# Two more units by seven products in an FFN output stage, another order, and an earlier look-ahead for the last weights

## The chip, the cores and the metric

The kernel runs on one core of a Trainium2 chip. The metric is the device time of one execution in microseconds; where several runs are given, their median counts.

## What is computed

One layer of a decoder: a sparse attention mixer, then a SwiGLU FFN, with RMSNorm ahead of each and at the end. The change lies in the second half of the FFN and in nothing else:

```python
def swiglu(h, w_in, w_out):          # h: 512 x 2048
    z = h @ w_in                     # w_in: 2048 x 11264
    a, b = z[..., :D_FF], z[..., D_FF:]
    return (jax.nn.silu(a) * b) @ w_out     # D_FF = 5632; w_out: 5632 x 2048
```

All data is float32. The kernel keeps float32 accuracy on TensorE by splitting each operand into a high part (rounded to the type that TensorE takes) and a low part (the rest), and adding three products: high by high, high by low, low by high. This is the helper `three`, lines 272 to 274, so every product appears as three matmuls.

## The kernel before

**Units.** The FFN output multiplies the gated activations `a` (512 tokens by 5632) by `w_out`. The 5632 rows are cut into 22 *pairs* of 2 x 128 rows, and the 2048 output columns into 4 *blocks* of 512. A *unit* is one pair in one block, 88 in all; `ORDER[b]` lists the pairs of block b in the order in which they are worked. TensorE goes through the units one after the other. In block 3 the last `N_TAIL` = 4 pairs of the order (17, 19, 20, 21) are held back: they are worked token tile by token tile at the very end, so that a finished tile can be normalised and stored while the next is multiplied.

**Two forms of a unit.** A plain unit (`plain_tile`, L1248) is 4 token tiles x 2 halves x 3 = 24 matmuls with 512 columns. A unit listed in `SEVEN[b]` (`seven_unit`, L1255) treats tokens and columns as a 2 x 2 block matrix and uses seven products of half size in place of eight, 42 matmuls with 256 columns. It needs sums of the activation's quarters and sums of the weight's quarters:

- The activation's side of a seven (seven quarter-sized matrices, high and low, tiles `ah` and `al`) is made once, by `form` (L1188), in the unit's first block. `form` is a generator of three steps, taken four, three and two units ahead of its unit; it reads the plain data by a SyncE transfer (`load_form`) into a part of `acc` that is not in use yet.
- The pairs in `KEPT` stay in SBUF for all blocks. The others are *passing*: `form` stores `ah` and `al` to DRAM (`d_s`, L1214, on the Pool queue), and later blocks fetch them back (`load_seven`, L1231, L1239, also on the Pool queue), 896 KB each. The pool `ast` has two buffers for passing pairs, so a fetch or a `form` waits until TensorE has left the passing pair before the last.
- The weight's side is made for every unit by `weight_sums` (L1125): four sums into the tile `tt`, then a split into `thi` and `tlo` (L1139 on ScalarE, L894 on VectorE), of which there are two buffers.

`merge_sums` (L1270) adds the four accumulators that the sevens of a block share into `acc`, once, in the unit after the block's last seven: one ScalarE copy and six VectorE instructions.

**Weights.** `W2` loads each unit's 512 KB of weights by SyncE (L77, tile `raw`, `RAW` = 3 buffers) and splits them into `whi` (ScalarE, L93) and `wlo` (VectorE, L95), in `CONV` = 4 buffers. `take(k)` sees to it that the weights of this unit and of the next k are split, and then issues loads for the next three that are not:

```python
    def ahead(self, n):
        last = len(self.specs)
        while self.ncv < min(self.nt + n, last):
            if self.nd <= self.ncv:
                self.load()
            self.split()
        while self.nd < min(self.ncv + RAW, last):
            self.load()
```

**Plain activations.** A plain unit's activation comes from DRAM (`d_a`) into one of two single buffers, `rawx` or `tt` (`load_a`, L1102, SyncE, L1108), and is split by `split_a` (L1110, L1116 on ScalarE, then L894). `tt` is the same tile in which `weight_sums` works, so a plain activation gets it only after the sums of the last seven ahead of it are split. For the last four pairs the split goes to `ah` and `al`.

**The order of the queues** is the order in which the program issues: each engine, and each DMA queue with it, works its instructions one after the other and waits where one has to wait. For one unit the loop of the output stage issues `W2.take`, then `split_a` up to the next unit (further ahead in the last two units before the held pairs), then `merge_sums` if it is due, the steps of `form`, the matmuls, `load_seven`, and one step of `ready`, which prepares the norm of the block before.

Of the kernel before, what the change touches and what calls it, by code (L numbers as in the profile page):

```python
# [29 lines left out]
N_PLAIN = 3  # L30
N_TAIL = 4
KEPT = (3, 8, 13, 16, 18)
SEVEN = [KEPT + x for x in ((6, 11), (6, 11, 0, 1, 2, 4)) + 2 * ((6, 11, 0, 1, 2, 4, 5, 7),)]
ORDER = [tuple(range(22)),
# [3 lines left out]
TP_GAP, HN_GAP = 40, 48  # L38
RESYNC = 14
SPREAD = 2560  # L40
# [128 lines left out]
def nsa_block(ctx: ExitStack, tc: tile.TileContext, x, rel_bias, mix_g, ffn_g, fin_g, w_in, w_out,  # L169
# [649 lines left out]
    def add(t, cb, p):  # L819
        a = acc[:, t, 512 * cb:512 * (cb + 1)]  # L820
        dve.tensor_tensor(a, a, p, op=OP.add)
# [13 lines left out]
    with tc.tile_pool(name="n2", bufs=1) as n2:  # L835
# [8 lines left out]
        for cb in (2, 3):  # L844
            po = out_tiles()
            for i in range(6):
                w = W.take(2 if cb == 2 else min(2 + i, 6))
# [206 lines left out]
    with tc.tile_pool(name="tmp", bufs=1) as tmp:  # L1054
# [10 lines left out]
        for p in range(N_PLAIN):  # L1065
            if p:
                pa = [ps3.tile([128, 512], F32, name="pp") for _ in range(2)]
                for i in range(4):
                    w = W.take()
# [17 lines left out]
    W2 = Weights(nc, rawp, convp, specs2)  # L1087
# [7 lines left out]
    for n, (b, j) in enumerate(seq):  # L1095
        home = "tt"
        if j not in SEVEN[b]:
            home = min(free, key=free.get)
# [11 lines left out]
    def split_a(n):  # L1110
        if n in held:
            if n >= NU - N_TAIL:
                h, l = (asl.tile([128, 1792], F32R, name=f"a{x}")[:, 48:48 + 2 * S] for x in "hl")
            else:
                h, l = (tp.tile([128, 1600], F32R, name=f"t{x}")[:, :2 * S] for x in ("hi", "lo"))
            act(h, a_raw[n], AF.Copy)  # L1116
            sub(l, a_raw.pop(n), f32(h))
            a_hl[n] = h, l
        elif n < NU:
            a_hl[n] = seven[seq[n][1]] if seq[n][1] in KEPT else passing.pop(0)  # L1120
        load_a(n)
# [3 lines left out]
    def weight_sums(n):  # L1125

        def first(r):
            b11, b12, b21, b22 = (r[:, 256 * i:256 * (i + 1)] for i in range(4))
            ttf = tp.tile([128, 1536], F32, name="tt", bufs=1)[:, :768]
            c0 = 0 if n and seq[n - 1][1] in SEVEN[seq[n - 1][0]] else 32  # L1130
            tt = ttf.rearrange("p (n c) -> p n c", n=3)
            sub(tt[:, 0], b22, b12)
            sub(b12, b12, b11)
            plus(tt[:, 1], tt[:, 0], b11)
            sub(tt[:, 2], b21, tt[:, 1])

            def rest():
                h, l = (tp.tile([128, 1600], F32R, name=f"t{x}")[:, c0:c0 + 768] for x in ("hi", "lo"))
                act(h, ttf, AF.Copy)  # L1139
                sub(l, ttf, f32(h))  # L1140
                t_hl[n] = [x.rearrange("p (n c) -> p n c", n=3) for x in (h, l)]

            return rest

        return first

    for n, (b, j) in enumerate(seq):
        if j in SEVEN[b]:
            W2.sums[n] = weight_sums(n)
# [25 lines left out]
    scratch = [acc[:, :, 1024:1536], acc[:, :, 1536:]]  # L1175
    forms = [n for n, (b, j) in enumerate(seq) if j in SEVEN[b] and (not b or j not in SEVEN[b - 1])]
    visits = [n for n, (b, j) in enumerate(seq) if j in SEVEN[b] and j not in KEPT]

# [52 lines left out]
    def load_seven(n):  # L1231

        while n_visit[0] < len(visits):
            v = visits[n_visit[0]]
            if v in forms or sum(x > n for x in visits[:n_visit[0]]) >= 2:
                break
            h, l = (ast.tile([128, 1792], F32R, name=f"a{x}") for x in "hl")
            for i, x in enumerate((h, l)):
                pool.dma_start(x.bitcast(F32), d_s[seq[v][1], i])  # L1239
            keep_seven(seq[v][1], h, l)  # L1240
            n_visit[0] += 1
# [6 lines left out]
    def plain_tile(n, w, t, first, last):  # L1248
        for k in range(2):
            ah, al = (x[:, S * k:S * (k + 1)][:, tok(t)] for x in a_hl[n])  # L1250
            three(po[t], ah, al, w[0][:, k], w[1][:, k], first and k == 0, last and k == 1)
# [3 lines left out]
    def seven_unit(n, w, first):  # L1255
        b = [[x[:, i, 256 * c:256 * (c + 1)] for x in w] for i in range(2) for c in range(2)]
        th, tl = t_hl.pop(n)
        right = dict(p1=b[0], p5=b[1], p2=b[2], p3=b[3], p7=(th[:, 0], tl[:, 0]), p6=(th[:, 1], tl[:, 1]),
                     p4=(th[:, 2], tl[:, 2]))
        for name in ("p7", "p6", "p1", "p5", "p2", "p3", "p4"):  # L1260
            for u in range(2):
                if name in qs:
                    o, new = qs[name][:, 256 * u:256 * (u + 1)], seq[n][1] == first and u == 0
                else:
                    o = po[2 * (name == "p4") + u][:, 256 * (name == "p3"):][:, :256]
                    new = not started and name != "p3"
                lh, ll = (x[:, L[name], 128 * u:128 * (u + 1)] for x in a_hl[n])
                three(o, lh, ll, *right[name], new, False)

    def merge_sums(b, qs):  # L1270

        c = slice(512 * b, 512 * b + 256), slice(512 * b + 256, 512 * b + 512)
        m = late2.tile([128, 1024], F32, name="m")
        u2, u3 = m[:, :512], m[:, 512:]

        def halves(x):
            return x.rearrange("p (u c) -> p u c", u=2)

        act(u3, qs["p1"], AF.Copy)
        plus(u2, u3, qs["p6"])  # L1280
        plus(acc[:, :2, c[0]], acc[:, :2, c[0]], halves(u3))
        plus(u3, u2, qs["p7"])
        plus(acc[:, 2:, c[0]], acc[:, 2:, c[0]], halves(u3))
        mm2 = m.rearrange("p (a c) -> p a c", a=2)
        plus(mm2, mm2, qs["p5"].unsqueeze(1).to_broadcast([128, 2, 512]))
        plus(acc[:, :, c[1]], acc[:, :, c[1]], m.rearrange("p (t c) -> p t c", t=4))

    def ready(b, gf):

        c = slice(512 * b, 512 * (b + 1))  # L1290
        for t in range(NT):
            junk = late2.tile([128, 1024], F32, name="m")[:, :512]
            act(junk, acc[:, t, c], AF.Square, accum_out=ss[t][:, b:b + 1])
            dve.tensor_tensor(acc[:, t, c], acc[:, t, c], gf, op=OP.mult)
            yield
# [3 lines left out]
    for b in range(4):  # L1299
        units = ORDER[b][:-N_TAIL] if b == 3 else ORDER[b]  # L1300
        po = [pf.tile([128, 512], F32, name=f"f{i}") for i in range(4)]
        qs = {x: pf.tile([128, 512], F32, name=f"f{i}") for i, x in enumerate(("p1", "p5", "p6", "p7"))}
        first7 = next(j for j in units if j in SEVEN[b])
        last7 = [j for j in units if j in SEVEN[b]][-1]
        started = False
        for i, j in enumerate(units):
            left = len(units) - 1 - i if b == 3 else 9
            w = W2.take(max(1, 3 - left))
            while na <= n + 1 + max(0, 2 - left):
                split_a(na)  # L1310
                na += 1
            if pending is not None:
                merge_sums(*pending)
                pending = None
            for k in (1, 2, 3, 4):
                next(forming.get(n + k, iter(())), None)
            if j in SEVEN[b]:
                seven_unit(n, w, first7)
            else:
                for t in range(NT):  # L1320
                    plain_tile(n, w, t, not started, b < 3 and i == len(units) - 1)
            started = True
            if j == last7:
                pending = b, qs
            load_seven(n)
            if i >= 4:
                next(todo, None)
            if i == 12:
                gf = late2.tile([128, 512], F32, name="gf")
                nc.sync.dma_start(gf, fin_g[None, 512 * b:512 * (b + 1)].to_broadcast([128, 512]))  # L1330
            n += 1
        if b < 3:
            for t in range(NT):
                add(t, b, po[t])
            todo = ready(b, gf)
# [50 lines left out]
```

## Time and profile before

| | |
|---|---|
| three runs | 2192.6, 2198.13, 2196.51 us; median 2196.51 |
| the profiled execution | 2191.91 us, span 2190.2 us |
| mean granted TensorE clock | 0.997 |
| output stage | from about 1724 us to the end of the span |

A row of a timeline gives the start in us from the span's start, the time of one instruction (or from the first to the last of several), the engine, the line, the operation, the tile written and the tiles read, and in brackets the idle time before it and what ended it. A row of waits gives who waited for whom, the sum in us, how often, and the longest. Engines: PE is TensorE (PEld its weight load), DVE VectorE, ACT ScalarE, POOL GpSimd, SP SyncE; SPq and POOLq are their DMA queues. Matmuls are pipelined, so what one costs is the distance to the start of the next. In the table by windows the columns are: the stretch, its length, the busy time of PE, PEld, DVE, ACT and POOL with the number of instructions, the granted TensorE clock, the share of the DMA engines, and GB/s.

### The profile page before, as it was taken

What the parts mean: (1) busy time and instruction counts of PE and PEld (TensorE: products, weight loads), DVE (VectorE), ACT (ScalarE), POOL (GpSimd) and SP (SyncE); (2) the same over time, 40 slices, a digit from 0 to 9 for tenths busy, and PEclk for the clock granted to TensorE, in tenths of its full rate; (3) what the DMA queues carried; (4) which work ended last, traced back from release to release, by engine and by line L of the source; (5) the groups of instructions that cost most, each with busy time, mean ns of one, the idle gap of its engine ahead of it and who ended that gap; (6) DMA issues with size and microseconds to landing.
All of it is one profiled execution on the core that took longest, in us unless ns stands there. A gap on an engine that the chain in (4) does not pass through costs nothing.

```text
span 2190.2 us, 37229 instructions
## 1 busy us (share of the span) xinstructions
PE 2146.6 (98%) x15154; PEld 1993.1 (91%) x15154; DVE 1564.2 (71%) x2564; ACT 935.7 (43%) x1447; POOL 121.4 (6%) x140
## 2 busy tenths in 40 slices
PE   6999999999999999999999999999999999999997
PEld 5889898888989888899999999999999888999996
DVE  5455565656645536698888888888888787877776
ACT  5343444544544324344444444344343454544344
POOL 3100000000013012000000000000000000001000
PEclk9999999999999999999999999999999999999999
DMA  5655232232263452244433333443334676878884
GB/s 168 208 142 164 77 97 87 83 96 88 92 211 106 164 178 101 97 145 126 130 121 126 126 118 125 126 135 126 120 122 132 243 280 217 293 273 309 303 302 150
DMA packets 240267, 345.18 MB, mean 158 GB/s; under 512 B 12991, under 2 KB 178911, under 8 KB 238944
## 3 DMA queue, kind: packets, MB, share of 16 engines
q1 hardware_dynamic: 225920, 269.39, 38.4%
q0 software_dynamic: 12880, 70.28, 8.3%
q10 hardware_dynamic: 1296, 3.15, 0.4%
q8 instruction: 118, 1.93, 0.4%
q14 instruction: 53, 0.43, 0.1%
HBM read 299.68 MB, written 48.34 MB: 159 GB/s over the span
## 4 chain that ended last, share of the span: by engine, by line
PE 93%; DVE 3%; DMA 2%; ACT 1%; issue 1%; SPq 0%; POOL 0%; ACTq 0%; DVEq 0%; POOLq 0%
PE f L274 18%; PE f L273 18%; PE f L272 18%; PE proj L272 8%; PE proj L274 8%; PE proj L273 8%; PE pt L739 2%; PE pp L274 1%; PE pp L272 1%; PE pp L273 1%; PE o L274 1%; PE o L273 1%; PE s L272 1%; PE s L274 1%; PE o L272 1%; PE s L273 1%
## 5 line engine op out<-in xcount | busy, mean ns | idle before, releaser
L95 DVE TENSOR_TENSOR wlo<-raw,whi 128x1024 fp32r<-128x1024 f32 (+1 forms) x208 | 252.6, 1217 | 142.9 <-ACT whi L93 141.9
L93 ACT ACTIVATE whi<-raw 128x1024 fp32r<-128x1024 f32 (+1 forms) x226 | 234.4, 1041 | 219.7 <-DVE raw L894 122.4
L894 DVE TENSOR_TENSOR tlo<-tt,thi 128x1536 fp32r<-128x1536 f32 (+2 forms) x134 | 195.9, 1462 | 110.8 <-ACT thi L996 88.7
L272 PE MATMUL f<-hn_h,whi 128*128 128x256 f32 x984 | 271.7, 276 | 0.7 <-ACT E L954 0.7
L273 PE MATMUL f<-hn_l,whi 128*128 128x256 f32 x984 | 271.6, 276 | 0.0
L274 PE MATMUL f<-hn_h,wlo 128*128 128x256 f32 x984 | 271.6, 276 | 0.0
L991 ACT ACTIVATE whi<-raw 128x1024 fp32r<-128x1024 f32 x123 | 126.1, 1057 | 292.4 <-DVE raw L894 282.1
L272 PE MATMUL proj<-hn_h,whi 128*128 128x512 f32 (+1 forms) x544 | 209.8, 386 | 1.0 <-DVE hn_l L261 1.0
L274 PE MATMUL proj<-hn_h,wlo 128*128 128x512 f32 (+1 forms) x544 | 207.1, 381 | 0.0
L273 PE MATMUL proj<-hn_l,whi 128*128 128x512 f32 (+1 forms) x544 | 206.7, 380 | 0.0
L272 PEld LDWEIGHTS f<-hn_h,whi 128*128 128x128 f32 x984 | 184.7, 188 | 1.1 <-ACT E L954 1.1
L274 PEld LDWEIGHTS f<-hn_h,wlo 128*128 128x128 f32 x984 | 184.7, 188 | 0.0
L273 PEld LDWEIGHTS f<-hn_l,whi 128*128 128x128 f32 x984 | 184.7, 188 | 0.0
L996 ACT ACTIVATE thi<-tt 128x1536 fp32r<-128x1536 f32 x82 | 121.8, 1486 | 84.6 <-PE f L273 75.9
L894 DVE TENSOR_TENSOR wlo<-raw,whi 128x1024 fp32r<-128x1024 f32 x123 | 147.0, 1223 | 0.0
L272 PE MATMUL proj<-whi,hn_h 128*128 128x256 f32 (+2 forms) x496 | 146.3, 295 | 0.0
L273 PE MATMUL proj<-wlo,hn_h 128*128 128x256 f32 (+2 forms) x496 | 145.2, 293 | 0.0
L274 PE MATMUL proj<-whi,hn_l 128*128 128x256 f32 (+2 forms) x496 | 145.0, 292 | 0.0
L298 DVE TENSOR_TENSOR ptl<-pt,pth 128x128 fp32r<-128x128 f32 (+3 forms) x128 | 62.5, 488 | 99.0 <-ACT pth L297 98.8
L274 PE MATMUL f<-whi,tlo 128*128 128x512 f32 x320 | 125.0, 391 | 0.7 <-DVE tlo L894 0.6
L273 PE MATMUL f<-wlo,thi 128*128 128x512 f32 x320 | 125.0, 391 | 0.0
L272 PE MATMUL f<-whi,thi 128*128 128x512 f32 x320 | 124.7, 390 | 0.0
(316 smaller groups left out, 6212.6 us busy)
## 6 DMA issues: line engine op xcount, KB each, us to landing
raw<-in_ffn_w_in SPq DMA_DIRECT2D x135, 512.0 KB, 3.5
raw<-in_ffn_w_out SPq DMA_DIRECT2D x88, 512.0 KB, 5.9
raw<-in_nsa_w_in SPq DMA_DIRECT2D x48, 512.0 KB, 3.6
rawx<-in_ffn_w_in SPq DMA_DIRECT2D x41, 512.0 KB, 4.9
rawx<-d_a SPq DMA_DIRECT2D x34, 512.0 KB, 5.1
raw<-in_nsa_w_out SPq DMA_DIRECT2D x32, 512.0 KB, 3.7
raw<-in_nsa_w_in SPq DMA_DIRECT2D x56, 256.0 KB, 3.3
ah<-d_s POOLq DMA_DIRECT2D x16, 896.0 KB, 7.0
```

The lines of the kernel that those rows point to most:

```text
L93: self.nc.scalar.activation(hi[:, :n], src, AF.Copy)
L95: eng.tensor_tensor(lo[:, :n], src, hi[:, :n].bitcast(F32), op=OP.subtract)
L272: mm(o, ah, bh, start=start, stop=False, skip_group_check=True)
L273: mm(o, ah, bl, start=False, stop=False, skip_group_check=True)
L274: mm(o, al, bh, start=False, stop=stop, skip_group_check=True)
L298: dve.tensor_tensor(lo, psum_ap, hi.bitcast(F32), op=OP.subtract)
L739: nc.tensor.transpose(pt[rows, 128 * (t - kt):128 * (t - kt + 1)], src, ident)
L894: dve.tensor_tensor(o, a, b, op=OP.subtract)
L991: act(h, r, AF.Copy)
L996: act(h, ttf, AF.Copy)
```

## The change

Pair 9 becomes a passing seven in blocks 2 and 3 (7, 11, 14 and 14 units by seven products in the four blocks, 46 where there were 44). The orders of blocks 2 and 3 are rearranged. In block 3 ahead of the held pairs, the weights are split two units ahead from four units before the end on (`left` is the number of units still to come before the held pairs), where this began only one unit before the end; the last step, three ahead in the last unit, stays.

```diff
 KEPT = (3, 8, 13, 16, 18)
-SEVEN = [KEPT + x for x in ((6, 11), (6, 11, 0, 1, 2, 4)) + 2 * ((6, 11, 0, 1, 2, 4, 5, 7),)]
+SEVEN = [KEPT + x for x in ((6, 11), (6, 11, 0, 1, 2, 4)) + 2 * ((6, 11, 0, 1, 2, 4, 5, 7, 9),)]
 ORDER = [tuple(range(22)),
          (3, 5, 6, 7, 0, 9, 8, 10, 1, 12, 11, 13, 14, 2, 16, 15, 17, 4, 18, 19, 20, 21),
-         (6, 9, 3, 11, 10, 5, 8, 12, 0, 13, 14, 1, 15, 7, 16, 2, 17, 18, 4, 19, 20, 21),
-         (6, 9, 3, 11, 10, 0, 8, 1, 12, 2, 13, 4, 14, 5, 16, 7, 18, 15, 17, 19, 20, 21)]
+         (6, 10, 3, 11, 12, 5, 8, 0, 14, 13, 7, 15, 1, 16, 2, 17, 18, 9, 4, 19, 20, 21),
+         (6, 10, 11, 3, 0, 8, 1, 12, 2, 13, 4, 16, 5, 14, 7, 18, 9, 15, 17, 19, 20, 21)]
...
             left = len(units) - 1 - i if b == 3 else 9
-            w = W2.take(max(1, 3 - left))
+            w = W2.take(3 if left == 0 else 2 if left < 5 else 1)
             while na <= n + 1 + max(0, 2 - left):
                 split_a(na)
                 na += 1
```

## The prediction

> **What bounds the kernel now.** I read the page first, then the waits of TensorE in the stretch of the FFN output (1700 us to the end), then the timelines of that stretch engine by engine.
>
> ```profile
> span 2190.2 us, 37229 instructions
> PE 2146.6 (98%) x15154; PEld 1993.1 (91%) x15154; DVE 1564.2 (71%) x2564; ACT 935.7 (43%) x1447; POOL 121.4 (6%) x140
> ```
> ```profile
> PE f L273 <- DVE wlo L95: 2.6, 1, 2.6
> PE f L274 <- DVE tlo L894: 0.6, 1, 0.6
> PE f L274 <- DVE al L894: 0.6, 1, 0.6
> PE f L274 <- DMA al<-d_s: 0.4, 1, 0.4
> ```
> TensorE is busy for 98% of the span. In the whole output stage it waits four times. The 0.6 behind tlo is at 1727, before anything that the diff touches. The change can therefore act in three places only: the matmul time itself, the 0.4 us behind a transfer, and the 2.6 + 0.6 us at the end.
>
> **Two pairs converted.** The three rows are the first matmul of a unit by seven products, of the plain unit after it, and of the next unit.
>
> ```profile
> 2006.40 0.28 PE L272 MATMUL f<-thi,ah 128*128 128x256 f32 x1
> ...
> 2011.25 0.40 PE L272 MATMUL f<-whi,thi 128*128 128x512 f32 x1
> ...
> 2016.73 0.28 PE L272 MATMUL f<-thi,ah 128*128 128x256 f32 x1
> ```
> Seven products (42 matmuls) take 4.85 us, a plain pair (24 matmuls) 5.48 us: 0.63 less. Pair 9 changes over in blocks 2 and 3, 44 units become 46: 2 x 0.63 = **-1.26 us**, all of it on the path, since TensorE is the path.
>
> What the conversion adds elsewhere must stay hidden. For each converted unit VectorE does four sums of 128x256 and a 768-wide tlo in place of one 1024-wide tlo. In block 2 pair 9 is also formed (four sums of 128x256 and three subtractions, spread over three units) and stored; in block 3 the Pool queue fetches its two stored halves (2 x 896 KB).
>
> ```profile
> L894 DVE TENSOR_TENSOR tt<-raw x7: 418/424/426, 2101.3 to 2135.3; 128x256 f32<-128x256 f32 x7
> ...
> 2137.90 0.28 PE L272 MATMUL f<-thi,ah 128*128 128x256 f32 x1
> ...
> 2138.15 0.85 ACT L1139 ACTIVATE thi<-tt 128x768 fp32r<-128x768 f32 x1 [0.91 <-PE f L274]
> ...
> 2139.03 0.96 DVE L894 TENSOR_TENSOR tlo<-tt,thi 128x768 fp32r<-128x768 f32 x1 [0.53 <-ACT thi L1139]
> ...
> 2158.86 1.22 DVE L95 TENSOR_TENSOR wlo<-raw,whi 128x1024 fp32r<-128x1024 f32 x1
> ```
> Per unit that is 4 x 0.42 + 1.22 + 0.96 = 3.9 us of 4.85. In a run of sevens the conversion for the next unit cannot start until TensorE leaves the unit before (thi waits for PE): pair 7 starts at 2137.90, thi at 2138.15, tlo is done at 2139.99, 2.1 us into the unit, and is needed 4.85 us into it. That leaves 2.8 us of slack. The new order is tightest in block 2 at pair 8: 3.9, one 128x512 step of the finished block (0.68, row of m below) and the first step of forming pair 7 (4 x 0.42 = 1.7), together 6.2 us, 1.4 over the unit. It fits in the 2.8. I take 0; if that cover went, the price is the overrun, 1.4 us.
>
> **The transfers of stored pairs.** Two buffers hold the passing pairs, so a fetch may start when the passing pair before the last one is done.
>
> ```profile
> al<-d_s POOLq DMA_DIRECT2D x16, 896.0 KB, 9.3
> ```
> ```profile
> 1970.01 0.54 POOL L1214 DMA_DIRECT2D d_s<-al  x1 [6.14 <-DVE al  L894]
> ```
> ```profile
> 2012.39 14.67 DMA al<-d_s
> ```
> In the new block 3 the nine passing pairs stand two units apart, so each fetch has three units: at least 3 x 4.85 = 14.6 us, against 5.48 + 2 x 4.85 = 15.2 or more before. The median landing is 9.3, with 0.5 us before it for the other half: a margin of 4.8. The one that was late (14.67, the 0.4 us wait) stood on the Pool queue behind the stores of the last formed pair and the residual. In the new order the last formed pair is 9, and the fetch of pair 4 stands ahead of its stores and of the residual: **-0.4 us**. The fetch of pair 0 in block 2 is the new narrow one: it stands right behind the stores of pair 5 (the row at 1970.01), and its window shrinks from four units to the same 15.2. A second late fetch like the longest row would cost 0.5 + 14.67 - 15.2 = 0. I take none.
>
> **The end.** These are TensorE, then the other queues, over the last units.
>
> ```profile
> 2152.89 0.39 PE L272 MATMUL f<-whi,ah 128*128 128x512 f32 x1
> ...
> 2157.07 0.49 PE L272 MATMUL f<-whi,ah 128*128 128x512 f32 x1
> 2160.14 0.49 PE L273 MATMUL f<-wlo,ah 128*128 128x512 f32 x1 [2.57 <-DVE wlo L95]
> 2161.27 0.50 PE L274 MATMUL f<-whi,al 128*128 128x512 f32 x1 [0.64 <-DVE al L894]
> ...
> 2161.84 0.62 PE L273 MATMUL f<-wlo,ah 128*128 128x512 f32 x1
> ...
> 2165.25 0.40 PE L272 MATMUL f<-whi,ah 128*128 128x512 f32 x1
> ```
> ```profile
> 2139.98 2.36 DVE L95 TENSOR_TENSOR wlo<-raw,whi 128x1024 fp32r<-128x1024 f32 x2
> ...
> 2145.53 1.22 DVE L894 TENSOR_TENSOR al<-tt,ah 128x1024 fp32r<-128x1024 f32 x1 [0.30 <-ACT ah L1116]
> ...
> 2152.56 1.23 DVE L894 TENSOR_TENSOR al<-tt,ah 128x1024 fp32r<-128x1024 f32 x1
> 2153.70 0.68 DVE L897 TENSOR_TENSOR m<-m,f 128x512 f32<-128x512 f32 x1
> ...
> 2157.72 1.22 DVE L897 TENSOR_TENSOR acc<-acc,m 128x1024 f32<-128x1024 f32 x1
> ```
> ```profile
> 2140.01 0.34 SPq L1108 DMA_DIRECT2D tt<-d_a  x1
> 2141.23 1.50 SPq L77 DMA_DIRECT2D raw<-in_ffn_w_out  x2
> ...
> 2146.78 0.34 SPq L1108 DMA_DIRECT2D tt<-d_a  x1
> ```
> ```profile
> 2140.01 4.40 DMA tt<-d_a
> ...
> 2146.78 4.66 DMA tt<-d_a
> ```
> The late wlo is the weights of pair 21, the last of the four held for the end. The chain behind it: the last seven's tlo frees the one tt buffer (2139.99); SyncE fetches pair 17 into it (2140.01, 4.40 us); ACT and VectorE split it; tt goes to pair 20 (2146.78, 4.66); split again, done 2153.78; then come the six instructions of merge_sums (2153.70 to 2158.94), and only behind them wlo of 21. TensorE issues L273 2.85 us late (2160.14, where 2157.07 + 0.22 was due) and the next 0.9 late.
>
> Now the change. The larger look-ahead moves the splitting of weights one unit forward at "4 left", but the chain starts with the *tlo* of the last seven, and that still waits for TensorE to leave the second unit before it: pair 7 for pair 9, as pair 16 for pair 18 until now. Between that moment and the four held pairs lie two sevens and pair 15, as before. So counted from there, the chain and its deadline stay as they were, and VectorE's order of steps from there on is the same. One thing moves, and the wrong way. Weight 15 is now split one unit earlier, and with it the load of weight 20 is issued one unit earlier on SyncE: ahead of pair 17's fetch into tt, where it stood behind it. That load needs the buffer that weight 15's wlo frees (before, the load at 2141.23 came at the end of the first wlo at 2139.98). So pair 17's fetch goes out behind it, at the place of 2141.23 + 0.34 instead of 2140.01: **1.56 us later**. It then has 512 KB ahead of it in its queue.
>
> ```profile
> 2154.00:2155.00 1.00, 1.00 (x6) 0.82 (x5) 0.99 (x2) 0.99 (x3) 0.00 (x0) 1.00 0.95 356
> ```
> At 356 GB/s (last column), 0.52 MB take 1.47 us, of which 0.34 have run: up to 1.1 more. Its second fetch has less beside it (4.40 instead of 4.66). Bounds: 1.56 - 0.26 = 1.3 if the load ahead costs nothing; 1.56 + 1.6 = 3.2 if it lands as slowly as the loads of 2141 did.
>
> ```profile
> raw<-in_ffn_w_out SPq DMA_DIRECT2D x1, 512.0 KB, 6.0
> ```
> (6.0 - 4.40 = 1.6.) I take 1.56 + 1.1 - 0.26 = 2.4, since the queue's order makes the upper half likelier than the lower. TensorE's deadline is unchanged, so this all shows: **+2.4 us**.
>
> **The clock.** After that wait the matmuls run at half rate.
>
> ```profile
> 876.28 0.39 PE L274 MATMUL pp<-hn_h,wlo 128*128 128x256 f32 x1 [2.67 <-DVE wlo L95]
> ```
> ```profile
> 2162.00:2163.00 1.00, 1.00 (x4) 0.81 (x3) 0.07 (x1) 0.00 (x0) 0.00 (x0) 0.50 0.00 0
> ```
> From 2161.84 to 2165.25 (3.41 us) the granted clock is 0.50: half of that, 1.7 us, is lost. A single wait of 2.67 at 876 was not followed by such a stretch. With the wait at about 5 us I expect one stretch again, change 0; bounds -1.7 (the clock falls during the wait and is back sooner) and +1.7 (two stretches). The Trainium skill (TensorE: Matmul & The Clock Gate, Part 1) says that the clock is halved after about one idle window of 3.4 us, windows that run on without regard to the kernel, and returns after a busy one. By that rule a longer wait still costs one window, change 0 as I took it. The length of the stretch agrees (3.41); that the wait before it, 2.57 us and a matmul later 0.64, is shorter than a window does not.
>
> **Sum**, on the profiled execution (2191.91 us, of which the span is 2190.2): -1.26 - 0.4 + 2.4 + 0 = +0.7, so 2192.6. That execution was quicker than the median of 2196.51 by 4.6, so on the median: 2196.5 + 0.7 = **2197.2 us**. Ends of the costs: -1.26 - 0.4 + 1.3 - 1.7 = -2.1 and -1.26 + 1.4 + 3.2 + 1.7 = +5.0.
>
> **Rivals.** *The look-ahead does cure the end.* Then 2.85 + 0.9 + 1.7 go, and with the other gains 7.1: 2189.4. For it: the edit is aimed at the loads before these four pairs. Against it: the late step hangs on the tt buffer and on merge_sums, which the look-ahead does not move. Chance 0.06.
>
> *Fetches of stored pairs become late: slower.* Nine in block 3 with 14.6 to 15.2 us, and in block 2 the fetches next to the stores of 5, 7 and 9. It decides once landing takes over 14.1 us from issue, so the median must rise by half, or the longest row must become the rule. If six fetches were 1 us late each: +6, with the forecast's +0.7 about 2203.2. Against it: the old order ran pairs two apart through block 3 without a wait at 15.2 us. For it: within the two blocks 2 x 512 KB of plain transfers go, and 512 KB for forming, 2 x 896 KB of stores and 2 x 896 KB of fetches come. Chance 0.16.
>
> *The two converted units help and nothing else moves* (the queue order does not matter): 2196.5 - 1.7 = 2194.8, chance 0.13; no change by the bound below. The forecast keeps 0.65.
>
> **Numbers.** A measurement of this kernel tells about 0.3% (6.6 us) from no change. Forecast and third rival lie within it, the first rival beyond it below (-7.1), the second mostly at or beyond it above. That gives 0.06 / 0.78 / 0.16. The three runs before spread over 5.5 us, so the medians alone may shift by 2 to 3. The range runs from 2191 (lower end of the costs and the spread) to 2203 (upper end, and the edge of the second rival).
>
> **What would show it.** In the changed profile: 46 units of 42 matmuls; no PE wait behind al<-d_s near the end of block 2; PE waits behind wlo at the end of 4.5 to 6 us instead of 2.6; on SyncE the last-but-one load of raw issued just ahead of tt<-d_a, and tt about 1.5 us later against the last seven's tlo; one stretch at half clock. Waits of PE behind al<-d_s in block 3 would make it wrong on the slow side; a wait behind wlo under 2 us at the end on the fast side.

## The result, and the profile after

| | before | after |
|---|---|---|
| median of 22 runs each | 2194.56 us (2190.56 to 2199.94) | 2200.64 us (2196.51 to 2206.72) |
| ratio to the kernel before | | 1.0027, 95% interval 1.0018 to 1.0035 |
| profiled execution, its span | 2191.91, 2190.2 us | 2198.5, 2196.8 us |
| granted clock | 0.997 | 0.994 |

The change costs 6 us. The forecast was 0.7 us. The time lies in the range and within the 0.3% that was called no change, but the interval shows a loss, and it is more than eight times as large as the sum. The question for the experiments is where the other 5 us come from.

TensorE's waits in the output stage of the kernel after (who waited for whom, sum in us, times, longest):

```profile
PE f L273 <- DVE wlo L95: 3.2, 1, 3.2
PE f L272 <- ACT thi L1116: 3.1, 1, 3.1
PE f L272 <- ACT ah L1116: 1.4, 1, 1.4
PE f L274 <- DVE tlo L894: 0.6, 1, 0.6
PE f L274 <- DVE al L894: 0.3, 1, 0.3
```

The wait behind `al<-d_s` is gone, as forecast. At the end 2.6 + 0.6 us have become 1.4 + 3.2 + 0.3. And there is a wait that no step of the prediction named: 3.1 us behind a `thi` of L1116, the split of a *plain* activation. TensorE's timeline of the kernel after shows where it lies:

```profile
2045.40 0.40 PE L272 MATMUL f<-whi,thi 128*128 128x512 f32 x1
...
2054.11 0.80 PE L272 MATMUL f<-whi,thi 128*128 128x512 f32 x1 [3.08 <-ACT thi L1116]
...
2055.96 0.63 PE L272 MATMUL f<-whi,thi 128*128 128x512 f32 x1
...
2067.88 0.39 PE L274 MATMUL f<-whi,tlo 128*128 128x512 f32 x1
```
```profile
2048.00:2052.00 4.00, 3.03 (x14) 2.18 (x12) 0.00 (x0) 0.00 (x0) 0.00 (x0) 1.00 1.03 417
2052.00:2056.00 4.00, 1.86 (x4) 1.04 (x5) 1.92 (x3) 2.49 (x3) 0.00 (x0) 0.66 1.01 409
2056.00:2060.00 4.00, 4.00 (x11) 3.13 (x10) 3.86 (x5) 0.28 (x1) 0.00 (x0) 0.50 0.73 288
```

These are the last three pairs of block 2 (19, 20, 21): 72 matmuls in a row from 2045.40 to 2067.88, 22.5 us. Without a wait the 71 distances of 0.227 make 16.1. So 6.4 us are lost here: 3.3 in the wait, the rest because the first three matmuls behind it start 0.6 us apart and the others 0.43 until 2060. The second fence (the table by windows) has the granted clock in its third column from the right: 0.66 in the mean of 2052 to 2056, then 0.50. In windows of 0.1 us it is 0.50 from 2053.3 to 2060.1: it fell 2.2 us after the last matmul ahead of the wait had ended. From 2048 to 2052, most of it ahead of the wait, VectorE, ScalarE and the Pool queue stand idle (0.00) while the DMA engines are at 1.03 of their time and 417 GB/s. A transfer is late, and the bandwidth is used up by others.

The chain of waits of the kernel after names it, and the timelines of SyncE and of the Pool queue show what went out beside it:

```profile
2037.99 14.90 DMA tt<-d_a
...
2145.76 6.15 DMA tt<-d_a
...
2154.28 3.48 DMA tt<-d_a
```
```profile
2027.49 9.66 SPq L77 DMA_DIRECT2D raw<-in_ffn_w_out  x3
2037.99 0.34 SPq L1108 DMA_DIRECT2D tt<-d_a  x1
...
2142.32 3.38 SPq L77 DMA_DIRECT2D raw<-in_ffn_w_out  x2
2145.76 1.57 SPq L1108 DMA_DIRECT2D tt<-d_a  x1
```
```profile
2026.44 0.53 POOL L1239 DMA_DIRECT2D ah<-d_s  x1 [19.03 <-PE f L274]
2026.95 0.53 POOL L1239 DMA_DIRECT2D al<-d_s  x1
2027.48 0.54 POOL L1214 DMA_DIRECT2D d_s<-ah  x1
2029.76 0.54 POOL L1214 DMA_DIRECT2D d_s<-al  x1 [1.75 <-DVE al L894]
2030.29 0.77 POOL L1183 DMA_DIRECT2D acc<-d_r  x1
2040.99 0.53 POOL L1239 DMA_DIRECT2D ah<-d_s  x1 [9.93 <-PE f L274]
```

Pair 20's plain load into `tt` (512 KB) goes out at 2037.99 and lands 14.9 us later. From 2026.44 to 2030.29 the Pool queue has issued a *burst*: the fetch of pair 4, the two stores of pair 9, which is formed here, and 1 MB of the residual. That residual is `load_residual`, line 1183, the last quarter of what is added to the FFN's output; the program issues it at the end of the last `form` of block 2. The fetches of pairs 6 and 11 for block 3 follow from 2040.99 on. In the kernel before the same stores and the residual stood well ahead of the plain load, which went out at 2039.78 and landed 5.8 us later:

```profile
2010.17 0.55 POOL L1214 DMA_DIRECT2D d_s<-al  x1 [5.57 <-DVE al L894]
2011.11 0.77 POOL L1183 DMA_DIRECT2D acc<-d_r  x1 [0.39 <-issue]
```
```profile
2039.78 0.34 SPq L1108 DMA_DIRECT2D tt<-d_a  x1
```
```profile
tt<-d_a SPq DMA_DIRECT2D x1, 512.0 KB, 5.8
```

The last formed pair was 7, six units ahead of pair 19; now it is 9, two units ahead. So the load, 29 us behind the residual before, is 8 us behind it now.

To compare profiles I cut the output stage in three, from a wait that all of them show early in it (behind `tlo`, at 1727.24 before and 1727.49 after) to the first of the last 120 matmuls, over these 120 (pair 15 and the four held pairs), and from the last matmul to the end of the span:

| us | to the last 120 | last 120 | behind | sum |
|---|---|---|---|---|
| before | 420.2 | 32.6 | 10.2 | 463.0 |
| after | 424.0 | 35.6 | 9.7 | 469.3 |

Of the +6.3, +3.8 arise ahead of the last units and +3.0 in them; 0.5 come back at the end. Each row is one execution. In that of the run with the loads on ScalarE's queue, TensorE waits 1.8 us at 1774 to 1782, ahead of anything that its edit touches; so a difference of 1 to 2 us in the first column can be chance.

### The profile page after: what moved, and what is told of

Its sections match the earlier page's. It is cut to its first block, busy times and chain, and to the rows that moved or that the text cites. A ratio compares the mean times of both kernels' runs of the same rounds, so it can differ in the third digit from the quotient of the medians.

```text
span 2196.8 us, 37326 instructions
## 1 busy us (share of the span) xinstructions
PE 2149.1 (98%) x15190; PEld 1996.0 (91%) x15190; DVE 1570.1 (71%) x2579; ACT 936.5 (43%) x1450; POOL 124.0 (6%) x144
## 3 DMA queue, kind: packets, MB, share of 16 engines
q10 hardware_dynamic: 1296, 3.15, 0.4%
## 4 chain that ended last, share of the span: by engine, by line
PE 94%; DVE 3%; DMA 2%; ACT 1%; issue 1%; SPq 0%; ACTq 0%; DVEq 0%
PE f L274 18%; PE f L272 18%; PE f L273 18%; PE proj L272 8%; PE proj L274 8%; PE proj L273 8%; PE pt L739 2%; DMA tt<-d_a 1%; PE pp L274 1%; PE pp L273 1%; PE pp L272 1%; PE o L274 1%; PE o L273 1%; PE s L272 1%; PE s L274 1%; PE o L272 1%
## 5 line engine op out<-in xcount | busy, mean ns | idle before, releaser
L272 PE MATMUL f<-whi,thi 128*128 128x512 f32 x304 | 119.8, 394 | 3.1 <-ACT thi L1116 3.1
L274 PEld LDWEIGHTS proj<-hn_h,wlo 128*128 128x128 f32 x544 | 103.6, 190 | 19.7
L272 PEld LDWEIGHTS proj<-hn_h,whi 128*128 128x128 f32 x544 | 103.9, 191 | 19.2 <-DVE hn_l L261 1.6
```

The lines of the kernel that those rows point to most:

```text
L272: mm(o, ah, bh, start=start, stop=False, skip_group_check=True)
L274: mm(o, al, bh, start=False, stop=stop, skip_group_check=True)
```

## The experiments

The theory is that two edits cost time at two places: the order puts the burst beside pair 20's load (about 6.4 us in block 2), and the look-ahead delays the load at the end (about 2.4). Rivals for block 2: the load is issued late; DMA bandwidth is shared by bytes, so that only less traffic helps; the look-ahead is to blame there too. The ratios are to the kernel before.

**The order without the look-ahead, and the look-ahead without the order.**

```diff
 # in the kernel after
-            w = W2.take(3 if left == 0 else 2 if left < 5 else 1)
+            w = W2.take(max(1, 3 - left))
```

> The changed kernel with the old look-ahead. Everybody expects the wait in block 2 (3.1 us behind thi of pair 20, then half clock) to stay, since no look-ahead acts there. My theory of the end (the load of weight 20 stands ahead of pair 17's fetch into tt): the end goes back to waits of about 2.6 and 0.6 us and tt is issued at the end of the last seven's tlo; about 2.9 us less than the changed kernel, 3.1 more than the kernel before (ratio 1.0014). Rival, that the end depends on the new order instead: end as in the changed kernel, ratio 1.0027.

> The kernel before with the new look-ahead alone. My theory of the end: no wait in block 2 beyond the old 0.4 us, and at the end 1.5 and 3.2 us of waits as in the changed kernel, so 2 to 3 us more than the kernel before (ratio 1.0009 to 1.0014). Rival, that the look-ahead only hurts with the new order: ratio 1.000 and the old waits at the end. Rival, that the look-ahead brings the gain it was aimed at: 2 us or more less.

The order with the old look-ahead: 2198.41 us, ratio 1.0017 (1.0008 to 1.0026). The wait in block 2 is there unchanged (3.10 us, the load landing 14.9 us after its issue), so the look-ahead has no part in it. The new look-ahead in the kernel before: 2196.49 us, 1.0012 (1.0003 to 1.0021), some 2.6 us slower. So the edit meant for the last pairs costs about 2 us by itself, near the 2.4 of the sum: 0.0012 alone (2.6 us), 0.0010 with the order (2.2), and 0.0008 (1.8) between the two kernels below in which the residual is moved and which differ in the look-ahead alone. The first has an interval of ±0.0009 and the two differences have wider ones; the sign is the same in all three, the size is rough. SyncE's timeline, first of the order alone, then of the look-ahead alone:

```profile
2145.00 0.34 SPq L1108 DMA_DIRECT2D tt<-d_a  x1
2146.22 1.50 SPq L77 DMA_DIRECT2D raw<-in_ffn_w_out  x2
```
```profile
2139.64 8.15 SPq L77 DMA_DIRECT2D raw<-in_ffn_w_out  x3
2147.84 0.46 SPq L1108 DMA_DIRECT2D tt<-d_a  x1
```

With the old look-ahead `tt` is issued at 2145.00, at the end of the last seven's `tlo` (2144.97), and the weights behind it. With the new one they stand ahead of it, and it goes out 1.66 us after that moment. What did not come as expected is the landing in the first of these kernels: 5.88 us, so its last 120 matmuls shrank by only 1.0 us. It is the exception. In the other seven kernels with the old look-ahead this transfer lands after 4.3 to 4.8 us, in the six with the new one after 5.3 to 6.5. Why it was late that one time is open.

**Less in the burst.** The residual's last quarter is issued four units into block 3.

```diff
 # in the kernel after
-        if i + 1 == len(forms):
-            load_residual(slice(1536, 2048))
...
+            if b == 3 and i == 4:
+                load_residual(slice(1536, 2048))
```

> The changed kernel, in which the last quarter of the residual (1 MB, Pool queue) is loaded in unit 4 of block 3 instead of behind the stores of the last formed pair. Theory S (SyncE's transfers, with their short rows, get a small share of the DMA engines while the Pool queue has work): the Pool queue is empty about 2.5 us earlier (1 MB at 410 GB/s), pair 20's plain load lands 2.5 us or more earlier, the wait of 3.1 us shrinks to under 0.7 and the half clock behind it goes: 5 to 6 us less than the changed kernel, ratio to before 1.000. Rival B (simply too many bytes, shared alike): about the same here. Rival L (the load goes out too late, because tt is held by the sums of the last seven): the wait stays at 3 us, ratio 1.0027.

2193.94 us, ratio 1.0004 (0.9995 to 1.0012): most of the loss is gone with one line moved. TensorE's waits, and the landing of the two plain loads in block 2 (2036 to 2056: KB, us):

```profile
PE f L273 <- DVE wlo L95: 3.2, 1, 3.2
PE f L272 <- ACT ah L1116: 1.0, 1, 1.0
PE f L274 <- DVE tlo L894: 0.9, 2, 0.6
PE f L274 <- DVE al L894: 0.3, 1, 0.3
```
```profile
tt<-d_a SPq DMA_DIRECT2D x1, 512.0 KB, 7.2
rawx<-d_a SPq DMA_DIRECT2D x1, 512.0 KB, 11.5
```

The 3.1 us behind `thi` are gone, and the waits of the end stand as they were. The load was issued 10.5 us behind the first store of pair 9 (2039.89 against 2029.37), as in the kernel after (2037.99 against 2027.48), and landed in 7.2 instead of 14.9 us. So it was not issued too late. The landing came 7.7 us earlier, where the 1 MB that was taken out is about 2.6 us of traffic at the 401 to 417 GB/s of the rows from 2040 to 2052 in the kernel after.

**The same bytes on another queue.** The plain loads of pairs 19, 20 and 21 in block 2 are issued on ScalarE's queue.

```diff
 # in load_a of the kernel after
-    nc.sync.dma_start(...)
+    (nc.scalar if n in (63, 64, 65) else nc.sync).dma_start(...)
```

> The changed kernel, in which the plain loads of pairs 19, 20 and 21 in block 2 are issued on ScalarE's queue instead of SyncE's; bytes, rows and the time from which the buffers are free stay. Theory Q (the DMA engines take turns between queues, and within a queue a load stands behind the weights ahead of it): pair 20's load lands in 6 to 9 us instead of 14.9, the 3.1 us wait goes or falls under 1; 4 to 6 us less than the changed kernel. Rival B (the burst's bytes shared alike by all transfers): it lands as late as before, 12 us or more, ratio 1.0027.

2194.25 us, ratio 0.9998 (0.9986 to 1.0011). Nothing was taken out of the traffic, and the wait of 3.1 us is gone (in this profile the burst lies 2.4 us later). The queues from 2028 to 2056 (packets, MB, share of the engines) and the landings, first of the kernel after, then of this one:

```profile
q0 software_dynamic: 1338, 7.89, 71.7%
q1 hardware_dynamic: 1307, 2.95, 28.7%
...
raw<-in_ffn_w_out SPq DMA_DIRECT2D x4, 512.0 KB, 13.3
...
tt<-d_a SPq DMA_DIRECT2D x1, 512.0 KB, 14.9
rawx<-d_a SPq DMA_DIRECT2D x1, 512.0 KB, 16.4
```
```profile
q0 software_dynamic: 1186, 6.92, 64.2%
q1 hardware_dynamic: 990, 1.93, 19.3%
q10 hardware_dynamic: 347, 1.22, 10.9%
...
raw<-in_ffn_w_out SPq DMA_DIRECT2D x5, 512.0 KB, 13.3
...
tt<-d_a ACTq DMA_DIRECT2D x1, 512.0 KB, 8.1
rawx<-d_a ACTq DMA_DIRECT2D x1, 512.0 KB, 8.4
```

q0 carries the Pool queue, q1 SyncE's and q10 ScalarE's. The load on the third queue lands in 8 us while the weights on SyncE's still take 13.3 in the median. So the plain load was slow for two reasons together: SyncE's queue gets 29% of the engines beside a full Pool queue, and the load stands in it behind three loads of weights. The theory by bytes alone falls. The second reason is the one that this run takes away: SyncE's and ScalarE's queues together have 30% of the engines, hardly more than the 29% of SyncE's alone. In the kernel after the two queues moved almost the same number of packets (1338 and 1307), of 5.9 and 2.3 KB on average: about one packet each in turn. The Trainium skill (DMA: Bandwidth & Descriptors, Queues, rings and completion order) states that each engine goes round its queues and works a whole packet before it turns to the next; the counts of this stretch agree, those of the kernel before from 2012 to 2040 (1267 on the Pool queue, 1649 on SyncE's, engines as busy) less.

**Shorter rows for the stored pairs.** If turns go by packets, smaller packets on the Pool queue should leave more for SyncE. The rows of a stored half, 7 KB, become 1.8 KB in a first kernel and 1 KB in a second.

```diff
 # in the kernel after, with the stores and fetches to match
-    d_s = dram.tile([NF // 2, 2, 128, 1792], F32, name="d_s")
+    d_s = dram.tile([NF // 2, 2, 4, 128, 448], F32, name="d_s")    # first kernel
+    d_s = dram.tile([NF // 2, 2, 7, 128, 256], F32, name="d_s")    # second kernel
```

> The changed kernel, in which the stored pairs lie in DRAM as four pieces of 448 columns, so that their stores and fetches go in rows of 1.8 KB instead of 7 KB; the bytes and all orders stay. Theory S: SyncE's loads in the burst land in 6 to 10 us instead of 12 to 17, the wait behind thi of pair 20 goes, the fetches of stored pairs take longer (12 us and more instead of 8 to 12); 5 to 6 us less than the changed kernel, ratio to before 1.000, unless the fetches become late themselves. Rival B: no less, the wait of 3 us stays or grows; ratio 1.0027 or more. Rival L: ratio 1.0027.

> As the run with rows of 1.8 KB, now seven pieces of 256 columns, rows of 1 KB. If the size of the Pool queue's rows sets SyncE's share: pair 20's load lands earlier again than the 12.3 us of that run, under 10, and the Pool queue's stores and fetches later; the wait goes, unless fetches become late. If the gain there was chance or came from something else: 12 to 15 us, and the wait as it was.

2195.78 us, 1.0013 (1.0004 to 1.0022), and 2198.94 us, 1.0014 (1.0002 to 1.0026). The load landed in 12.3 and 11.4 us; 6 to 10 had been expected of the first. SyncE's queue in the same stretch:

```profile
q1 hardware_dynamic: 1405, 3.20, 31.2%
```
```profile
q1 hardware_dynamic: 1389, 3.20, 31.2%
```

By these rows the share rose from 28.7 to 31.2%, and not further with 1 KB than with 1.8 KB. But the burst of the second kernel begins 1.6 us later than that of the kernel after. Over 28 us from the same distance behind each burst's first fetch, the shares are 28.7, 31.0 and 32.5%, with Pool packets of 5.9, 4.7 and 3.8 KB in the mean. So the smaller packets did go with a larger share, but the rows became four and seven times shorter and the packets only 1.3 and 1.5 times smaller. The packet counts also drift apart (1561 to 1405 and 1683 to 1389 in the rows' stretch). The wait of 3.1 us is gone in both, in favour of waits of 0.4 to 1.2 us in block 2. What is shown is that a load on a queue of its own does not stand behind another queue's loads, and that less work on the Pool queue helps by more than its bytes; by what unit the engines divide their time is not shown.

**The end: merge_sums behind the first plain tiles.** In the kernel before, wlo of pair 21 stands behind the 5.2 us of `merge_sums` on VectorE. Here block 3's `merge_sums` moves behind the last four pairs' products of token tile 0, where its result is first needed.

```diff
 # in the kernel before
-            if pending is not None:
+            if pending is not None and not (b == 3 and left == 0):
                 merge_sums(*pending)
...
+        if t == 0:
+            merge_sums(*pending)
         add(t, 3, po[t])
```

> The kernel before, with merge_sums of block 3 issued behind the splits of the four held pairs instead of ahead of them. If the wait at the end comes from the six instructions of merge_sums standing ahead of pair 21's wlo, the two waits there (2.6 and 0.6 us) and the stretch at half clock go: 4 to 5.5 us less, ratio 0.9975 to 0.998. Rival, that the plain loads into tt and rawx set the end: the waits stay, now behind ah or al; ratio 1.000.

2193.72 us, 0.9994 (0.9982 to 1.0006); 0.9975 to 0.998 had been expected. The wait is cured: the last 120 matmuls take 28.6 us instead of 32.6. But 13.0 us pass from the last matmul to the end, 2.8 more than before: VectorE starts on the finished tiles late and each tile's finishing takes it and ScalarE about 5.1 us, against 5.4 of TensorE's, so the backlog is hardly worked off. Another 2 us went into a late fetch (1.9 behind `al<-d_s`) in this profile; that wait is 0.4 in the kernel before, the edit does not touch it, and why it was longer here is open.

**Together.** The order with the old look-ahead, the residual later and merge_sums behind; then the parts of it.

> The changed kernel with the old look-ahead, the residual's last quarter in unit 4 of block 3, and merge_sums of block 3 behind the splits of the held pairs. If the two conversions are worth their 1.3 to 1.7 us once the waits are gone: 1 to 2 us less than the kernel before with merge_sums moved alone, ratio to before 0.997 to 0.9975. If the burst of transfers in block 2 still costs what they bring: no less than that kernel.

> The kernel before with the residual's last quarter in unit 4 of block 3. In its trace the fetch of pair 2 stands behind that residual and TensorE waits 0.4 us for it. If the conversions and the old look-ahead are what makes the combined version quicker: only that wait goes here, 0 to 1 us less, ratio 0.9995 to 1.000. Rival, that the moved residual is most of the combined version's gain: 3 us or more less, ratio under 0.9987.

> The changed kernel with the old look-ahead and the residual's last quarter in unit 4 of block 3; merge_sums as it was. If the two costs of the change add up and are all there is: the kernel before less the two conversions, 1 to 2 us less, ratio 0.999 to 0.9997, and less than the run with the residual moved alone by the 2 us of the look-ahead. Rival, that the order of blocks 2 and 3 costs something else: ratio 1.0003 or more.

> The kernel before (44 units by seven products, its own order, its own look-ahead), with the two edits that need nothing of the change: the last residual load at unit 4 of block 3, and merge_sums of the last block behind the plain tiles of the first output tile. It is the combination kernel without the change's two conversions and order. Theory 1 (once the two stalls are gone, the conversions are worth what TensorE saves, 1.3 to 1.7 us on a profile): ratio to the kernel before 0.9978 to 0.9988, and the combination kernel in the same call 0.6 to 2 us below it. Theory 2 (the new order or the burst still costs what the conversions save): equal to the combination kernel within 0.5 us. Theory 3 (moving merge_sums gives little on the old order, as with the single edit: 0.9994): 0.999 or more, and the combination kernel 3 us or more below it. In the profile: no wait behind wlo at the end, 120 last matmuls in 27.5 to 29 us, 12.5 to 13 us from the last matmul to the end of the span.

> The combination kernel once more (46 units and the new order, the old look-ahead, the residual at unit 4 of block 3, merge_sums behind the first plain tiles), on the same chip as the kernel before with the last two of these edits. If its 0.9974 was no chance of that chip, it gives 0.9965 to 0.9983 again.

| kernel | median, us | ratio (95%) | to the last 120 | last 120 | behind | sum |
|---|---|---|---|---|---|---|
| before + residual later | 2193.96 | 0.9996 (0.9986 to 1.0005) | 419.5 | 32.6 | 10.2 | 462.3 |
| before + residual later + merge_sums behind | 2192.43 | 0.9995 (0.9986 to 1.0004) | 419.9 | 27.9 | 13.0 | 460.9 |
| order, old look-ahead, residual later | 2193.72 | 0.9996 (0.9986 to 1.0006) | 419.6 | 32.6 | 9.7 | 461.8 |
| the combination | 2189.3 | 0.9974 (0.9963 to 0.9984) | 418.9 | 28.0 | 12.6 | 459.4 |
| the combination again | 2190.11 | 0.9985 (0.9975 to 0.9995) | 419.2 | 27.8 | 12.6 | 459.6 |

The combination is faster than both kernels, by 5.7 us in the first comparison and 3.3 in the second (just less than was expected of it). The kernel before with the residual and merge_sums moved gave 0.9995, where 0.9978 to 0.9988 had been expected if the parts add up; its profile shows the parts, its device times do not show their sum. In the profiles the combination is 3.5 us shorter than the kernel before, and there the parts add up: the residual 0.7, merge_sums 1.4 (without the conversions) to 2.4 (with them), the two conversions with their order 0.5 to 1.5. In device time the last of these is 2.3 us in medians, 0.0010 between two ratios whose intervals are each about ±0.001: its sign is likely, its size is not settled, and the profiles with their 1 to 2 us of chance do not settle it either. The waits that are left to the combination:

```profile
PE f L274 <- DVE tlo L894: 1.2, 2, 0.6
PE f L274 <- DVE al L894: 0.5, 1, 0.5
PE f L272 <- ACT thi L1116: 0.4, 1, 0.4
```

## Why the prediction was right, and where it was not

That the time lies in the range is luck. The upper end of the costs was +5.0, and the loss is 6. From the median of the 22 runs before, that end would lie at 2199.6, and 2200.64 was measured. The range still held it because the three runs that it starts from lay 2 us higher, and because it was widened to the edge of a rival.

**Two conversions, -1.26: right, a little more.** In blocks 2 and 3 of the kernel after, 28 sevens take 134.2 us; in the kernel before, 26 take 124.9 without their one wait. So two more cost 9.3 us and replace 2 x 5.48 = 11.0: -1.7. The first seven of a run takes 4.85 us as quoted, one behind another seven only 4.75 to 4.77, and the new order has longer runs. A run of five in block 3, from its first matmul to the first of the plain unit behind it, shows it (23.9 us, 4.78 each):

```profile
2078.44 0.28 PE L272 MATMUL f<-thi,ah 128*128 128x256 f32 x1
...
2102.34 0.40 PE L272 MATMUL f<-whi,thi 128*128 128x512 f32 x1
```

The added work on VectorE cost nothing, as taken: no wait behind `tlo` or `wlo` appears in these blocks.

**The transfers of stored pairs, -0.4: that wait went, but the step failed.** "I take none" was right for the fetches: none of block 3 is late. It was the wrong question. The step asked whether each *fetch* still has time, and put down the move of pair 9's stores and of the residual as a gain, since nothing on the Pool queue stands behind them any more. It did not ask what they collide with at their new place, 8 us ahead of a plain load on *another* queue, behind three loads of weights, with the fetches for block 3 to come. That is the burst of 2026 to 2030, and it costs 6.4 us; the runs with the residual moved and with the load on ScalarE's queue each took it away. The quoted row of a transfer that took 14.67 us on the Pool queue was the warning: it was read as that queue's order alone, though the DMA engines were full there (0.97 to 1.03 of their time from 2012 to 2024), and the weights that SyncE loaded beside it landed after 10.7 us in the median (2003 to 2025). The removed wait had cost 0.6, with its slower matmuls, not 0.4.

**The end, +2.4: right in its steps, near in size.** `tt` goes out behind the load of weight 20, 1.66 us after the last seven's `tlo` (1.56 forecast; the row at 2145.76 in SyncE's timeline above), and lands in 6.15 instead of 4.40 us (+1.75, where +1.1 was taken and 1.6 was the bound). The second fetch gained more than was taken (3.48 instead of 4.66). Counted from the start of the third-last unit ahead of the held pairs, `al` of pair 20 is done after 18.1 us, where it was 15.9: +2.2. On the device the look-ahead costs 1.8 to 2.6 us, with the uncertainty said above. The wait came in another shape than the step had it, 1.4 behind `ah` and 3.2 behind `wlo` in place of 4.5 to 6 behind `wlo`: TensorE was held up earlier in the chain. VectorE's timeline of the kernel after, with that `tlo` and the `wlo` of pair 21 behind `merge_sums`:

```profile
2143.14 0.96 DVE L894 TENSOR_TENSOR tlo<-tt,thi 128x768 fp32r<-128x768 f32 x1 [0.84 <-ACT thi L1139]
2144.08 2.36 DVE L95 TENSOR_TENSOR wlo<-raw,whi 128x1024 fp32r<-128x1024 f32 x2
...
2165.17 1.22 DVE L95 TENSOR_TENSOR wlo<-raw,whi 128x1024 fp32r<-128x1024 f32 x1
```

**The clock, 0: near in price at the end, wrong in its account.** The step expected one stretch of 3.41 us at the end. The granted clock is 0.50 there from 2165.9 to 2172.7, which is 6.8 us or two such stretches, the upper bound of the step. Part of it lies in the waits, so that only 0.7 us more were lost than before. The same holds in every profile in which `merge_sums` was not moved: one stretch of 3.4 us where the wait behind `wlo` was 2.5 to 2.6 us (three kernels), 6.8 where it was 3.15 to 3.17 (seven kernels). And there is another place at half rate, around the new wait in block 2, again 6.8 us (2053.3 to 2060.1); half of the loss of 6.4 us there is the clock. The rule that the prediction cites from the Trainium skill (TensorE: Matmul & The Clock Gate, Part 1) counts one idle window of 3.4 us; the single wait of 3.08 us in block 2 was shorter, and the clock fell 2.2 us into it. That the windows run on without regard to the kernel agrees: from 2060.1 to 2165.9 are 31 times 3.41 us.

**The sum.** -1.7 - 0.6 + 6.4 + 2.2 + 0.7 - 0.5 = +6.5, against +6.3 in the stage by the table. Without the burst it would have been about 0, and the forecast of +0.7 would have been close. The run with the order and look-ahead as they are and only the residual moved, at 1.0004, bears this out. Of the rivals, the second had the sign and the kind of cause (transfers that become late near the stores of 9), but named the wrong transfer: not six fetches by 1 us each, but one plain load by 3.1 and the clock with it.

## What to carry to other kernels

When a step that issues DMAs is moved, write down what goes out within 15 us of its new place on *all* queues, and where the DMA engines are full, look for the in-order queue that gets the small share: its loads are the ones that come late, not those of the queue that fills it. Here a load that fed TensorE next did better on a queue of its own than behind weights that were needed later. A look-ahead that is grown moves loads ahead of others in the same queue; look which of them is needed first.

## What the hardware showed that was not expected

- Beside a full Pool queue, SyncE's queue got 29% of the DMA engines' time, and its 512 KB loads took 12 to 17 us, where the medians of the whole kernel are 5.0 (`rawx`) and 5.8 (weights); the same load on ScalarE's queue took 8.
- Stalls cost about twice their length where the clock follows: 3.08 us of waiting made 6.4 us, while the wait of 1.9 us in block 2 of the kernel with merge_sums behind was followed by no half rate. The half rate lasted 3.4 us or 6.8 us, and it could begin inside the wait.
- Work taken off the path ahead of the last matmul came back behind it: 4.7 us gained, 2.8 paid, because each tile's finishing takes nearly as long as its multiplication.
